# First mixer's parameter stage, attention probabilities and layer norms of a two-layer trunk: four edits to the order and the engines of small operations

## The chip, the cores and the metric

The kernel runs on one core of a Trainium2 chip. A core has five engines that run side by side, each through its own queue in a fixed order: TensorE (PE in the rows, its weight loads PEld) multiplies, VectorE (DVE), ScalarE (ACT) and GpSimd (POOL) work elementwise, and SyncE (SP) issues most of the transfers. Engines wait for each other by semaphores. The metric is the time of one execution on the device, in microseconds (us); lower is better. The time of the kernel before is the median of 3 runs.

## What is computed

Two layers over 512 tokens of width 1024, each a mixer and a mixture of experts, with a layer norm behind each of the four.

```python
for layer in range(2):
    mix = fox_s5_mixer(h, ...) if layer == 0 else mlstm_mixer(h, ...)
    h = layer_norm(ALPHA * h + mix, ln_g[layer, 0], ln_b[layer, 0])
    h = layer_norm(ALPHA * h + hier_moe(h, ...), ln_g[layer, 1], ln_b[layer, 1])

def fox_s5_mixer(x, ...):
    q, k, v, f_logit, u = split(x @ w_in)          # 512, 512, 512, 8, 512 columns
    att = forgetting_attention(q, k, v, f_logit + f_bias)   # 8 heads of 64
    y = gelu(s5_scan(u, ...))                      # 32 groups of 16 channels, 64 states
    y = y * sigmoid(y @ w_glu + b_glu)
    return concatenate([att, y]) @ w_out

# forgetting_attention: c = cumsum(log_sigmoid(f_logit)); s = q k^T / 8 + c_q - c_k, causal;
#                       p = softmax(s);  out = p v
# s5_scan: h_t = lam * h_{t-1} + B u_t,  y = Re(C h) + D u,  lam = exp(dt * a) complex
# layer_norm: (x - mean) * rsqrt(var + 1e-5) * g + b
```

## The kernel before

All large products are made of three passes over parts: each operand is split into a high part (ScalarE's cast, L213) and a low part (VectorE or GpSimd subtracts, L214), and `mm3` (L266 to L268) adds high x high, high x low and low x high. Weights come in pieces of 1 MB (`load_piece`); a piece is loaded into one raw buffer, split, and used. The tile framework gives out the buffers: tiles of one tag share a fixed number of slots ("t" has 5, "s5pw" 2, "raw" 1). A planner sets the order of each engine's queue when the program is built, by the order in the source among what it holds ready, so that an operation's place in the source is its priority; on the chip each queue runs in that order, and an operation that waits holds up those behind it.

`mixer0` (L389) runs the first mixer. It loads x, projects u (two pieces, L401 to L412) and stores it, and then traces `s5_params` (L413, body L542 to L671): VectorE computes, in some 150 small operations of 32 to 128 columns that depend on one another, the discretised S5 parameters. Within it `powers` (L625) builds the first eight powers of a complex number by doubling, 18 operations a call: once for the state (PR, PI; L641) and twice for a rotation (C_, S_; L656 to L662), whose tables only lines 752 to 757 read, on GpSimd. Behind it come the forget gate: its weights are loaded and split by `small_w` (L415, L357), 24 products make the gate's rows (`gate_rows`), and VectorE and ScalarE make log-sigmoid and its running sum (L420 to L424), which the attention scores read. Then the four S5 batches are traced as generators and v is projected (two pieces). A batch's first phase makes parameters and outer products (L685 to L705; for batch 0 on VectorE, for the others mostly on GpSimd), transposes them (L717), makes small products (L732, L733), and the rotation C, S of 512 columns (L752 to L757, GpSimd). The second phase (L762 to L782) applies rotation and scan, and makes y.

`fox_pair` (L464) runs two heads: q and k projection, and for each head and each block of 128 queries the scores (L482 to L486), the row maximum (L488, VectorE), the exponential with its row sum (L491, ScalarE), the reciprocal (L492) and the product with it (L493, both VectorE). Then TensorE transposes the probabilities (L500), which are split and multiplied by v.

`out_proj` ends a mixer: 4 blocks of 128 tokens, products, the residual, statistics (`ln_stats`), the router, and `ln_apply` (L295), which applies the norm in two halves of 512 columns, two operations each (L300, L301). The MoE follows. `moe` (L1269) ends it: for each of 4 token blocks the last experts' parts are added to the gathered row (L1284, with a row sum), then `ln_sums` (L303), a generator of three steps: the mean (L309); squares of both halves on ScalarE with row sums (L314), variance, `rstd` on GpSimd (a power, L281), mean times rstd (L319); and the normalisation: ScalarE scales (L323), VectorE multiplies by g (L324), VectorE or GpSimd adds b (L325, by `LN_POOL`), each by halves. The result goes to `done`: behind the first MoE the transposes and splits for the second mixer (L1041), at the end the stores (two for a block). Behind block 0 of the first MoE a weight piece is split whose two operations are placed behind `last_act` and `last_ln`.

Of the kernel before, what the change touches and what calls it, by code (L numbers as in the profile page):

```python
# [11 lines left out]
BF16 = mybir.dt.bfloat16  # L12
I32 = mybir.dt.int32
AF = mybir.ActivationFunctionType
ALU = mybir.AluOpType
# [5 lines left out]
EPS = 1e-5  # L21
# [4 lines left out]
QK_AT = 1, 3  # L26
LN_POOL = (), (0,), (0,), ()
NLAST = 2
# [23 lines left out]
class Trunk:  # L52
# [242 lines left out]
    def ln_apply(self, y, gb, mu, rs):  # L295
        V = self.nc.vector
        g, b = gb
        for i in range(2):
            h = np.s_[:, i * 512:(i + 1) * 512]
            V.scalar_tensor_tensor(y[h], y[h], mu, g[h], op0=ALU.subtract, op1=ALU.mult)  # L300
            V.scalar_tensor_tensor(y[h], y[h], rs, b[h], op0=ALU.mult, op1=ALU.add)  # L301

    def ln_sums(self, y, s, gb, pool):  # L303

        nc = self.nc
        V = nc.vector
        g, b = gb
        mu = self.sm("lnmu", [128, 1], bufs=4)
        V.tensor_scalar(mu, s[:, 0:1], s[:, 1:2], -1.0 / 1024, op0=ALU.add, op1=ALU.mult)  # L309
        yield  # L310
        q = self.sm("lns", [128, 2], bufs=4)
        for i in range(2):
            junk = self.t("t", [128, 512])
            nc.scalar.activation(junk, y[:, i * 512:(i + 1) * 512], AF.Square, bias=mu, accum_out=q[:, i:i + 1])  # L314
        ve = self.sm("lnve", [128, 1])
        V.tensor_scalar(ve, q[:, 0:1], q[:, 1:2], 1.0 / 1024, op0=ALU.add, op1=ALU.mult)
        V.tensor_scalar(ve, ve, EPS, None, op0=ALU.add)
        rs = self.rstd(ve)
        V.tensor_tensor(mu, mu, rs, op=ALU.mult)  # L319
        yield  # L320
        for i in range(2):
            h = np.s_[:, i * 512:(i + 1) * 512]
            self.last_act = nc.scalar.activation(y[h], y[h], AF.Identity, scale=rs, bias=mu)  # L323
            self.last_ln = V.tensor_tensor(y[h], y[h], g[h], op=ALU.mult)  # L324
            (nc.gpsimd if i in pool else V).tensor_tensor(y[h], y[h], b[h], op=ALU.add)  # L325
        yield
# [62 lines left out]
    def mixer0(self):  # L389
# [13 lines left out]
        for half in range(2):  # L403
# [4 lines left out]
            for c in range(2):  # L408
# [3 lines left out]
                nc.sync.dma_start(ud[half * 2 + c].rearrange("s p j -> p s j"), us)  # L412
        self.s5_params()  # L413

        fw = self.small_w("fw", 8)  # L415
        fps = self.gate_rows(fw, x, 8)
        fb = self.sm("gb", [8, 1], bufs=1)
# [46 lines left out]
    def fox_pair(self, pr, x, v, cneg):  # L464
# [7 lines left out]
        for hh in range(2):  # L472
# [4 lines left out]
            for qb in range(4):  # L477
# [14 lines left out]
                nc.vector.reciprocal(r, r)  # L492
                nc.vector.tensor_scalar(p_[:, :n], p_[:, :n], r, None, op0=ALU.mult)  # L493
                P.append(p_)
# [47 lines left out]
    def s5_params(self):  # L542
# [81 lines left out]
        V.tensor_scalar(ZI, ZI, -1.0, None, op0=ALU.mult)  # L624
        def powers(R_, I_):  # L625

            m = 1
            while m < 8:
                t1 = self.sm("s5pw", [128, 4, 32], bufs=2)[:, :m, :]
                t2 = self.sm("s5pw", [128, 4, 32], bufs=2)[:, :m, :]  # L630
                kr = R_[:, m:m + 1, :].to_broadcast([128, m, 32])
# [24 lines left out]
        for i in range(2):  # L656
            C_, S_ = keep(9), keep(9)
            nc.gpsimd.memset(C_[:, 0, :], 1.0)
            nc.gpsimd.memset(S_[:, 0, :], 0.0)
            V.tensor_copy(C_[:, 1, :], co)  # L660
            V.tensor_copy(S_[:, 1, :], ss)
            powers(C_, S_)  # L662
            co, ss = C_[:, 8, :], S_[:, 8, :]
            CS.append((C_, S_))
# [604 lines left out]
    def moe(self, layer, done):  # L1269
# [3 lines left out]
        for tb in range(6):  # L1273
            if tb < 4:
                x = self.xr[tb]
                s = self.sm("lnsm", [128, 2], bufs=4)
                for n in range(2):
                    ns = np.s_[n * 512:(n + 1) * 512]
                    ps = self.p("pj" if n == 0 else "mm", [128, 512])
                    for i in range(NLAST):  # L1280
                        for j in range(2):
# [3 lines left out]
                                                   accum_out=s[:, n:n + 1])  # L1285
                ln.append(self.ln_sums(x, s, gb, LN_POOL[tb]))
                next(ln[tb])
# [311 lines left out]
```

## Time and profile of the kernel before

| | |
|---|---|
| time, median of 3 runs | 1134.22 us (1133.0 to 1135.67) |
| profiled execution, its own time | 1129.98 us |
| its span | 1127.9 us |
| mean granted TensorE clock | 0.966 |
| TensorE busy | 1022.9 us, 91% |
| VectorE busy | 815.3 us, 72% |
| ScalarE busy | 559.5 us, 50% |
| GpSimd busy | 379.6 us, 34% |
| moved from and to memory | 180.62 MB, mean 160 GB/s |

The span runs from the first to the last instruction of the profiled execution; 2.1 us of its time lie around it. In it the first mixer takes about 310 us, the first MoE until about 560 us with its norms, the second mixer until about 870 us, and the second MoE the rest. All starts in the rows are in us from the span's start. In a row "out<-in" names the tile that is written and those that are read, buffer numbers left out; "[3.20 <-ACT pt L213]" says that the engine stood idle 3.20 us before it and what ended that. Busy TensorE is modelled time and not TensorE at its peak.

### The profile page before, as it was taken

How to read it: one execution, taken by the hardware profiler on the slowest of the kernel's cores; microseconds unless marked ns; L12 is line 12 of the kernel's file. 1: busy time of each engine (PE TensorE's matmuls, PEld its weight loads, DVE VectorE, ACT ScalarE, POOL GpSimd, SP SyncE). 2: the span in 40 equal slices, each digit the busy share in tenths (PEclk: the TensorE clock that was granted, in tenths of full speed). 3: DMA queues.
4: the chain of work that ended last, by engine and by line, in shares of the span. 5: the costliest groups of instructions: out<-in, count | busy, mean ns of one | idle time of the engine just before them, and what ended most of it. 6: DMA issues, size and time to landing. Idle time of an engine off the chain costs nothing. (4 is left out here: it accounts for less than half of the span.)

```text
span 1127.9 us, 14810 instructions
## 1 busy us (share of the span) xinstructions
PE 1022.9 (91%) x5522; PEld 826.9 (73%) x5522; DVE 815.3 (72%) x1485; ACT 559.5 (50%) x778; POOL 379.6 (34%) x226
## 2 busy tenths in 40 slices
PE   7879999999989999997699999999999899999872
PEld 5566767767768787875577989898777787877761
DVE  7886899778776776767665766667988767767666
ACT  5123554461445665664544444444424556666744
POOL 3077546001223333345243333331012233424352
PEclk9899999999989999999799999999999899999986
DMA  6313321541257786768622222221402577868684
GB/s 227 104 58 109 127 66 46 170 170 37 114 211 249 274 291 233 287 240 248 144 75 75 76 75 75 75 76 38 150 38 114 178 267 274 313 226 297 226 218 134
DMA packets 48347, 180.62 MB, mean 160 GB/s; under 512 B 17588, under 2 KB 18516, under 8 KB 32264
## 3 DMA queue, kind: packets, MB, share of 16 engines
q1 hardware_dynamic: 41240, 156.11, 39.4%
q0 software_dynamic: 2992, 8.77, 4.0%
q10 hardware_dynamic: 4032, 14.68, 3.2%
q8 instruction: 46, 0.75, 0.3%
q14 instruction: 37, 0.30, 0.1%
HBM read 155.94 MB, written 22.42 MB: 158 GB/s over the span
## 5 line engine op out<-in xcount | busy, mean ns | idle before, releaser
L266 PE MATMUL pj<-x,wh 128*128 128x512 f32 x288 | 116.6, 406 | 7.4 <-ACT x L213 5.7
L214 POOL TENSOR_TENSOR wl<-raw,wh 128x2048 fp32r<-128x2048 f32 x15 | 69.9, 4663 | 137.2 <-ACT wh L213 137.2
L267 PE MATMUL pj<-x,wh 128*128 128x512 f32 x288 | 115.5, 401 | 0.0
L214 POOL TENSOR_TENSOR wl<-ca,wh 128x2048 fp32r<-128x2048 f32 x16 | 75.1, 4692 | 119.9 <-ACT wh L213 97.5
L213 ACT CAST wh<-raw 128x2048 fp32r<-128x2048 f32 (+1 forms) x49 | 88.2, 1801 | 53.4 <-DMA raw<-in_w 40.0
L268 PE MATMUL pj<-x,wl 128*128 128x512 f32 x288 | 114.7, 398 | 0.0
L1073 PEld LDWEIGHTS tp<-t,a 128*128 128x128 f32 x896 | 110.8, 191 | 3.0 <-ACT pt L1065 0.6
L1073 PE MATMUL tp<-t,a 128*128 128x256 f32 x896 | 111.8, 283 | 0.0
L214 POOL TENSOR_TENSOR x<-ca,x 128x2048 fp32r<-128x2048 f32 x14 | 64.6, 4618 | 135.7 <-ACT x L213 106.2
L214 DVE TENSOR_TENSOR wl<-raw,wh 128x2048 fp32r<-128x2048 f32 (+1 forms) x34 | 72.8, 2140 | 39.6 <-ACT wh L213 39.3
L214 DVE TENSOR_TENSOR wl<-ca,wh 128x2048 fp32r<-128x2048 f32 x14 | 32.1, 2292 | 60.7 <-ACT wh L213 60.7
L1180 ACT ACTIVATE a<-mm,s5bc 128x512 f32<-128x512 f32 x56 | 38.5, 687 | 73.4 <-PE mm L268 73.4
L213 ACT CAST x<-ca 128x2048 fp32r<-128x2048 f32 (+1 forms) x40 | 66.1, 1651 | 12.3 <-DMA ca<-in_w 8.4
L266 PEld LDWEIGHTS pj<-x,wh 128*128 128x128 f32 x288 | 55.4, 192 | 19.7 <-ACT x L213 6.8
L267 PEld LDWEIGHTS pj<-x,wh 128*128 128x128 f32 x288 | 54.8, 190 | 12.0 <-DVE x L214 1.8
L213 ACT CAST wh<-ca 128x2048 fp32r<-128x2048 f32 x30 | 57.1, 1904 | 13.0 <-DMA ca<-in_w 12.9
L268 PEld LDWEIGHTS pj<-x,wl 128*128 128x128 f32 x288 | 55.1, 191 | 10.7
L1054 DVE TENSOR_SCALAR t<-iota,rcm 128x128 fp32r<-128x128 f32 x112 | 58.5, 565 | 0.4
L267 PE MATMUL pj<-wl,x 128*128 128x256 f32 x192 | 56.4, 294 | 0.9 <-DVE wl L214 0.9
L268 PE MATMUL pj<-wh,x 128*128 128x256 f32 x192 | 56.2, 293 | 0.1
L266 PE MATMUL pj<-wh,x 128*128 128x256 f32 x192 | 56.2, 293 | 0.0
L281 POOL TENSOR_TENSOR lnrs<-lnve,nhalf 128x1 f32<-128x1 f32 x16 | 13.1, 818 | 126.3 <-DVE lnve L292 99.7
(488 smaller groups left out, 2869.1 us busy)
## 6 DMA issues: line engine op xcount, KB each, us to landing
raw<-in_w SPq DMA_DIRECT2D x63, 1024.0 KB, 5.2
ca<-in_w SPq DMA_DIRECT2D x62, 1024.0 KB, 5.8
yd<-a ACTq DMA_DIRECT2D x28, 512.0 KB
a<-in_ln SPq DMA_DIRECT2D x8, 512.0 KB, 6.5
a<-in_w SPq DMA_DIRECT2D x6, 512.0 KB, 6.8
yd<-t SPq DMA_DIRECT2D x6, 512.0 KB, 3.1
ca<-in_xT SPq DMA_DIRECT2D x8, 256.0 KB, 5.7
xr<-in_x SPq DMA_DIRECT2D x4, 512.0 KB, 6.3
```

The lines of the kernel that those rows point to most:

```text
L213: a = nc.scalar.copy(h, src)
L214: b = (eng or nc.vector).tensor_sub(l, src, h.bitcast(F32))
L266: nc.tensor.matmul(ps, lhsT=aH[ai], rhs=bH[bi], start=first, stop=False)
L267: nc.tensor.matmul(ps, lhsT=aH[ai], rhs=bL[bi], start=False, stop=False)
L268: nc.tensor.matmul(ps, lhsT=aL[ai], rhs=bH[bi], start=False, stop=last)
L281: self.last_pow = self.nc.gpsimd.tensor_tensor(rs, ve, self.nhalf, op=ALU.pow)
L1054: ins = nc.vector.tensor_scalar(oh[:, j, m * 128:(m + 1) * 128], self.iota1, c[2 * i + j], None, op0=ALU.is_equal)
L1073: nc.tensor.matmul(tp[:, k, :], lhsT=self.xs[tb][i][:, cs], rhs=ohs[tb], start=tb + i == 0, stop=tb + i == 4)
L1180: nc.scalar.activation(yo[:, ns], ps, AF.Copy, scale=c)
```

## The change

Four edits. (1) In `mixer0` the load and split of the forget gate's weights are traced ahead of `s5_params` instead of behind it; the products and the rest of the gate stay behind. (2) In `s5_params` the two calls of `powers` for the rotation, and the two copies ahead of each, go from VectorE to GpSimd; their temporaries come from tag "t" (5 slots) in place of "s5pw" (2 slots). The call for the state's powers stays. (3) In `fox_pair` the product of the probabilities with the reciprocal goes from VectorE to ScalarE, a Copy with a scale. (4) The norms are applied at full width: `ln_apply` with two operations of 1024 columns in place of four of 512. In `ln_sums` one square of 1024 columns (into a bf16 scratch tile) takes the place of two; VectorE makes (y - mean) * g as soon as the square has read y; the variance takes one small operation; and the last step is one VectorE operation, y * rstd + b. ScalarE's scaling, the product of mean and rstd, and GpSimd's sums go. `last_act` now names the square and is set in the second step.

```diff
--- before.py
+++ after.py
@@ -24,7 +24,6 @@
 TWO_PI = 6.283185307179586
 S5_AT = 1, 1, 2
 QK_AT = 1, 3
-LN_POOL = (), (0,), (0,), ()
 NLAST = 2
 
 
@@ -295,12 +294,10 @@
     def ln_apply(self, y, gb, mu, rs):
         V = self.nc.vector
         g, b = gb
-        for i in range(2):
-            h = np.s_[:, i * 512:(i + 1) * 512]
-            V.scalar_tensor_tensor(y[h], y[h], mu, g[h], op0=ALU.subtract, op1=ALU.mult)
-            V.scalar_tensor_tensor(y[h], y[h], rs, b[h], op0=ALU.mult, op1=ALU.add)
-
-    def ln_sums(self, y, s, gb, pool):
+        V.scalar_tensor_tensor(y, y, mu, g, op0=ALU.subtract, op1=ALU.mult)
+        V.scalar_tensor_tensor(y, y, rs, b, op0=ALU.mult, op1=ALU.add)
+
+    def ln_sums(self, y, s, gb):
 
         nc = self.nc
         V = nc.vector
@@ -308,21 +305,15 @@
         mu = self.sm("lnmu", [128, 1], bufs=4)
         V.tensor_scalar(mu, s[:, 0:1], s[:, 1:2], -1.0 / 1024, op0=ALU.add, op1=ALU.mult)
         yield
-        q = self.sm("lns", [128, 2], bufs=4)
-        for i in range(2):
-            junk = self.t("t", [128, 512])
-            nc.scalar.activation(junk, y[:, i * 512:(i + 1) * 512], AF.Square, bias=mu, accum_out=q[:, i:i + 1])
+        q = self.sm("lns", [128, 1], bufs=4)
+        junk = self.t("t", [128, 1024], BF16)
+        self.last_act = nc.scalar.activation(junk, y, AF.Square, bias=mu, accum_out=q)
+        V.scalar_tensor_tensor(y, y, mu, g, op0=ALU.add, op1=ALU.mult)
         ve = self.sm("lnve", [128, 1])
-        V.tensor_scalar(ve, q[:, 0:1], q[:, 1:2], 1.0 / 1024, op0=ALU.add, op1=ALU.mult)
-        V.tensor_scalar(ve, ve, EPS, None, op0=ALU.add)
+        V.tensor_scalar(ve, q, 1.0 / 1024, EPS, op0=ALU.mult, op1=ALU.add)
         rs = self.rstd(ve)
-        V.tensor_tensor(mu, mu, rs, op=ALU.mult)
         yield
-        for i in range(2):
-            h = np.s_[:, i * 512:(i + 1) * 512]
-            self.last_act = nc.scalar.activation(y[h], y[h], AF.Identity, scale=rs, bias=mu)
-            self.last_ln = V.tensor_tensor(y[h], y[h], g[h], op=ALU.mult)
-            (nc.gpsimd if i in pool else V).tensor_tensor(y[h], y[h], b[h], op=ALU.add)
+        self.last_ln = V.scalar_tensor_tensor(y, y, rs, b, op0=ALU.mult, op1=ALU.add)
         yield
 
 
@@ -410,9 +401,9 @@
                 us = self.t("t", [128, 8, 64])
                 nc.scalar.copy(us, ps.rearrange("p (j s) -> p s j", s=8))
                 nc.sync.dma_start(ud[half * 2 + c].rearrange("s p j -> p s j"), us)
+
+        fw = self.small_w("fw", 8)
         self.s5_params()
-
-        fw = self.small_w("fw", 8)
         fps = self.gate_rows(fw, x, 8)
         fb = self.sm("gb", [8, 1], bufs=1)
         nc.sync.dma_start(fb, self.I["fb"])
@@ -490,7 +481,7 @@
                 r = self.sm("foxr", [128, 1], bufs=4)
                 nc.scalar.activation(p_[:, :n], sc[:, :n], AF.Exp, bias=mx, accum_out=r)
                 nc.vector.reciprocal(r, r)
-                nc.vector.tensor_scalar(p_[:, :n], p_[:, :n], r, None, op0=ALU.mult)
+                nc.scalar.activation(p_[:, :n], p_[:, :n], AF.Copy, scale=r)
                 P.append(p_)
             po = self.p("sm", [64, 512])
             for kb in range(4):
@@ -622,12 +613,12 @@
         V.tensor_tensor(a1, a1, a2, op=ALU.subtract)
         V.scalar_tensor_tensor(ZI, a1, sgn2, den, op0=ALU.mult, op1=ALU.mult)
         V.tensor_scalar(ZI, ZI, -1.0, None, op0=ALU.mult)
-        def powers(R_, I_):
+        def powers(R_, I_, V=V, tag="s5pw"):
 
             m = 1
             while m < 8:
-                t1 = self.sm("s5pw", [128, 4, 32], bufs=2)[:, :m, :]
-                t2 = self.sm("s5pw", [128, 4, 32], bufs=2)[:, :m, :]
+                t1 = self.t(tag, [128, 4, 32])[:, :m, :] if tag == "t" else self.sm(tag, [128, 4, 32], bufs=2)[:, :m, :]
+                t2 = self.t(tag, [128, 4, 32])[:, :m, :] if tag == "t" else self.sm(tag, [128, 4, 32], bufs=2)[:, :m, :]
                 kr = R_[:, m:m + 1, :].to_broadcast([128, m, 32])
                 ki = I_[:, m:m + 1, :].to_broadcast([128, m, 32])
                 V.tensor_tensor(t1, R_[:, 1:m + 1, :], kr, op=ALU.mult)
@@ -657,9 +648,9 @@
             C_, S_ = keep(9), keep(9)
             nc.gpsimd.memset(C_[:, 0, :], 1.0)
             nc.gpsimd.memset(S_[:, 0, :], 0.0)
-            V.tensor_copy(C_[:, 1, :], co)
-            V.tensor_copy(S_[:, 1, :], ss)
-            powers(C_, S_)
+            nc.gpsimd.tensor_copy(C_[:, 1, :], co)
+            nc.gpsimd.tensor_copy(S_[:, 1, :], ss)
+            powers(C_, S_, nc.gpsimd, "t")
             co, ss = C_[:, 8, :], S_[:, 8, :]
             CS.append((C_, S_))
 
@@ -1283,7 +1274,7 @@
                                              start=i + j == 0, stop=i == NLAST - 1 and j == 1)
                     nc.vector.scalar_tensor_tensor(x[:, ns], ps, 1.0, x[:, ns], op0=ALU.mult, op1=ALU.add,
                                                    accum_out=s[:, n:n + 1])
-                ln.append(self.ln_sums(x, s, gb, LN_POOL[tb]))
+                ln.append(self.ln_sums(x, s, gb))
                 next(ln[tb])
             if 0 < tb < 5:
                 next(ln[tb - 1])
```

## Rows read from the trace of the kernel before

**Rows 1.** The page's part 1: busy us (share of span) xinstructions.

```profile
PE 1022.9 (91%) x5522; PEld 826.9 (73%) x5522; DVE 815.3 (72%) x1485; ACT 559.5 (50%) x778; POOL 379.6 (34%) x226
```

**Rows 2.** TensorE's waits, 36 to 60, 60 to 80: total, times, longest.

```profile
PE sm L266 <- ACT pt L213: 3.2, 1, 3.2
PE sm L268 <- DVE pt L214: 1.9, 1, 1.9
...
PE tp L717 <- DVE xr L705: 3.0, 1, 3.0
PE sm L733 <- DVE xr L705: 4.0, 2, 3.3
```

**Rows 3.** TensorE by stretch: busy (instructions), granted clock, DMA share, GB/s.

```profile
43.00:50.00 7.00, 7.00 (x22) 0.65 0.41 151
```

**Rows 4.** Timeline, SyncE and ScalarE: start, us, engine line operation [idle before].

```profile
32.56 0.52 SPq L360 DMA_DIRECT2D t<-in_fw  x1
...
37.15 1.90 ACT L213 CAST wh<-raw 128x2048 fp32r<-128x2048 f32 x1 [9.69 <-DMA raw<-in_w]
...
39.43 0.25 ACT L213 CAST pt<-t 128x64 fp32r<-128x64 f32 x1
```

**Rows 5.** VectorE, 22 to 52, groups by shape: busy us, mean ns.

```profile
L633 DVE TENSOR_TENSOR s5pw<-raw 128x128 f32<-128x128 f32 x3 | 0.9, 286 | 0.1
...
L633 DVE TENSOR_TENSOR s5pw<-raw 128x32 f32<-128x32 f32 x3 | 0.6, 185 | 0.0
```

**Rows 6.** Timelines of GpSimd and VectorE; all engines from 36 to 78.

```profile
51.18 0.99 POOL L724 TENSOR_TENSOR s5pw<-ident,s5d 16x128 f32<-16x128 f32 x1 [30.14 <-DVE raw L638]
...
58.40 1.72 POOL L752 TENSOR_TENSOR s<-raw 128x512 f32<-128x512 f32 x1
...
76.63 0.40 POOL L689 TENSOR_TENSOR s5pw<-s5bc,raw 128x128 f32<-128x128 f32 x1
76.99 1.11 POOL L701 TENSOR_TENSOR xr<-raw,s5A 128x512 f32<-128x512 f32 x1
...
36.79 0.17 DVE L660 COPY raw<-s5t 128x32 f32<-128x32 f32 x1
...
58.84 1.84 DVE L705 TENSOR_TENSOR xr<-xr,pt 128x512 f32<-128x512 f32 x1
...
78.83 2.41 DVE L703 TENSOR_TENSOR pt<-raw,s5Aw 128x512 f32<-128x512 f32 x2 [3.65 <-POOL s5Aw L690]
...
81.76 1.28 DVE L705 TENSOR_TENSOR xr<-xr,pt 128x512 f32<-128x512 f32 x2
...
36.00:78.00 42.00, 29.71 (x197) 22.44 (x196) 35.06 (x79) 11.48 (x15) 20.74 (x19) 0.88 0.26 83
```

**Rows 7.** Lines 493, 491: ns min/median/max, first and last start; 110 to 240.

```profile
L493 DVE TENSOR_SCALAR t<-t,foxr x32: 254/422/1512, 107.8 to 232.5; 128x128 f32<-128x128 f32 x8, 128x256 f32<-128x256 f32 x8, 128x384 f32<-128x384 f32 x8, 128x512 f32<-128x512 f32 x8
...
L491 ACT ACTIVATE t<-mm,foxm x32: 351/532/692, 106.8 to 231.4; 128x128 f32<-128x128 f32 x8, 128x256 f32<-128x256 f32 x8, 128x384 f32<-128x384 f32 x8, 128x512 f32<-128x512 f32 x8
...
110.00:240.00 130.00, 124.07 (x720) 91.29 (x719) 110.02 (x226) 69.99 (x151) 49.00 (x47) 1.00 0.33 106
```

**Rows 8.** Lines 300 and 1197: the same operation, half and full width.

```profile
L300 DVE SCALAR_TENSOR_TENSOR xr<-xr,lnmv,a x16: 740/743/748, 257.9 to 866.5; 128x512 f32<-128x512 f32 x16
...
L1197 DVE SCALAR_TENSOR_TENSOR xr<-a,xr x8: 1207/1212/4797, 501.9 to 1072.2; 128x1024 f32<-128x1024 f32 x8
```

**Rows 9.** Behind the first MoE: TensorE's timeline, and all engines from 580 to 840.

```profile
554.34 1.12 PE L1041 MATMUL tp<-ident,xr 128*128 128x128 f32 x4 [5.86 <-DVE xr L325]
...
580.00:840.00 260.00, 257.07 (x1368) 215.64 (x1366) 182.75 (x258) 116.46 (x176) 66.57 (x16) 0.99 0.22 77
```

**Rows 10.** The end: VectorE's timeline, and all engines by stretch.

```profile
1109.38 0.69 DVE L1284 SCALAR_TENSOR_TENSOR xr<-pj,xr 128x512 f32<-128x512 f32 x1 [0.73 <-DMA xr<-yd,rsrc]
...
1123.09 1.28 DVE L325 TENSOR_TENSOR xr<-xr,a 128x512 f32<-128x512 f32 x2
...
1101.99:1124.37 22.38, 5.01 (x21) 3.49 (x19) 17.97 (x46) 11.83 (x24) 5.24 (x6) 0.67 0.45 124
```

## What the change is expected to do

> **What bounds the kernel now.** I read the busy shares first, then what TensorE waits for by stage, and then the stage around each edit. TensorE is busy for 1022.9 of 1127.9 us [rows 1], so an edit is worth what it takes out of TensorE's waits, or out of the end, where TensorE is already done. In the first 80 us it waits for four things [rows 2]: 3.2 us for the high part of the forget-gate weights, 1.9 us for their low part, and 3.0 and 4.0 us for the S5 products (L705). [...] The S5 stage is therefore worth at most 3.2 + 1.9 + 2.4 + 3.0 + 4.0 = 14.5 us. From 110 to 240 us, the attention, TensorE is busy for 124.1 of 130 us [rows 7], so at most 5.9 us can be won there. From 580 to 840 us it is busy for 257.1 of 260 [rows 9]: what is gained ahead of that stage is carried through it. At the very end VectorE is busy for 17.97 of 22.38 us [rows 10], while no product is left to run.
>
> **Part 1, forget-gate weights ahead.** The load was issued at 32.56 us and its high part was made only at 39.43, right behind a 1.90 us cast that had waited until 37.15 for another transfer [rows 4]. That first operation needs nothing of the S5 parameters, so an earlier place removes both waits and the clock loss, 7.5 us, if the load does get issued before the second v piece. The moved step issues one load (SyncE), one cast and one subtraction; they pass the S5 chain on VectorE, where the subtraction is one more small operation (0.2 us).
>
> **Part 2, rotation powers on GpSimd.** Two of the three sets of 18 operations leave VectorE. One set is six operations each at 0.286 us (128 wide), about 0.22 (64 wide, estimated between its neighbours) and 0.185 (32 wide) [rows 5], 4.1 us; two sets and four copies are about 9 us, and as they run back to back with some overlap I take 8 us off VectorE ahead of the S5 products of batch 0. GpSimd sat idle for 30.1 us up to 51.18 [rows 6], so it has room. Its price is not in the trace for 32 wide. A 128-wide product took 0.40 us undisturbed and a 512-wide one 1.11 [rows 6], a slope of 1.85 ns an element, so 0.28 for 64 and 0.22 for 32; 12 x (0.40 + 0.28 + 0.22) = 10.8 us, with four copies at 0.2 and some 0.05 between dependent operations 13.6 us. Disturbed it is longer: next to GpSimd's 1.72 us product at 58.40, VectorE's L705 took 1.84 us [rows 6], where two of the same line took 1.28 together at 81.76, with GpSimd idle [rows 6]. The two engines' products take turns. From 36 to 78 us VectorE ran 79 operations in 35.1 us [rows 6]; without the 40 that leave and the dozen small ones at its start, and undisturbed, I put what meets the rotation at 26 operations and some 16 us, so GpSimd's bounds are 13.6 and 13.6 + 16 = 29.6 us; I take the middle, 22. The rotation starts where its first copy stood, 36.79 [rows 6], and ends at 50 to 66, for me at 58.5. Its first reader on GpSimd, L752, began at 58.40 before [rows 6]: so the rotation tables C and S come no sooner and no later.
>
> [...]
>
> **What that leaves of the 14.5 us.** VectorE reaches batch 0's products 8 us or more earlier, so TensorE's 3.0 and 4.0 us waits go. But batch 1's parameters run on GpSimd behind L752 to L757, and there VectorE already waited 3.65 us at 78.83 (L703) for them [rows 6]. With C and S at the same time as before, batch 1's products are not earlier either. TensorE would arrive at batch 1's transposes up to 14.5 us early and must then do something else. What it has is pair 0's q and k projection, 48 products of 0.23 us spacing, 11 us, if the planned order puts them there. Bounds: 0 (it waits for batch 1) and 12. I take 5, because some of this projection already stood ahead of that point, and because nothing in the trace shows how the planner will order it. The chain of the forget gate now draws its "t" buffers behind the twelve that GpSimd's powers use, so VectorE's L420 may come some 5 us later; its reader, pair 0's scores, has its first exponential at 106.8 [rows 7], so I cost it at nothing. Queued behind L420 on VectorE are batch 0's products and the v parts: if that cover fails, it costs up to those 5 us, inside the bounds.
>
> **Part 3, probabilities by ScalarE.** 32 operations leave VectorE, median 0.422 us, 13.5 us in all; 32 come onto ScalarE, priced like its exponentials of the same widths, median 0.532 [rows 7], 17 us. ScalarE was busy for 70.0 of the 130 us, VectorE for 110.0 [rows 7]: there is room. Each new operation waits on ScalarE for VectorE's reciprocal, with casts out of PSUM queued behind it, for which TensorE waits. Gain at most some 2 us of the 5.9, loss at most some 32 x 0.1 = 3 us. I take 0.
>
> **Part 4, full-width norms in the middle.** Two halves of 0.743 us become one of 1.21 [rows 8], two such pairs in a block: 2 x (1.486 - 1.21) = 0.55 us on the last block's chain, in two layers: 1 us.
>
> **Part 5, norms behind the first MoE.** TensorE waited 5.86 us until 554.34 for block 0 [rows 9]. Its chain was two squares of half the width with their read-outs, two small operations, the power on GpSimd, another small one, ScalarE's scaling, product and sum. It becomes one square, a product of 1.21 that VectorE can do while it waits for a gather, one small operation, the power, and a last 1.21. That is about 1 to 3 us sooner, and the weights' low part behind it, too. I take 2.2; the stage from 580 us carries it [rows 9].
>
> **Part 6, the end.** The last gather lands at 1109.38; VectorE's last operation ends 15 us later, at 1124.37, and the store takes 3.5 us to 1127.9 [rows 10]. VectorE's work hardly changes: eight full-width operations (9.3 us at 1.16 spacing) for eight products and six sums (8.4). What goes is the detour over ScalarE and GpSimd's sums, for which VectorE stood idle 4.4 of the 22.38 us. [...] So 10.5 to 13.5 us in place of 15.0, minus 0.5 as the last store no longer goes in two steps: gain 1 to 4.5, I take 3.3.
>
> **The sum.** 5 + 0 + 1 + 2.2 + 3.3 = 11.5 us off the profiled execution's 1129.98, 1118.5. The median of the runs is 4.2 us above that execution; I carry it: 1123 us, with its own range 1117 to 1129.
>
> **Rivals.** (a) All of the S5 stage's waits go, for GpSimd ends its powers near 50 us and batch 1 moves up too: 12 in place of 5, 1116 us. For it: 30.1 us of idle GpSimd [rows 6]. Against: its products take turns with VectorE's. (b) The first mixer gives nothing, since TensorE only waits for batch 1 at a later place; the norms' 6.5 us remain: 1128 us. For it: the 3.65 us wait that is there already [rows 6]. (c) Slower: the powers and VectorE's 512-wide products take strict turns. Then each of 40 operations costs 0.40 + 0.60 = 1.0 us, the powers end near 77, and L752 is 18 us late. I let GpSimd's short gaps behind it give back 3; batch 1 and TensorE at its transposes are 15 us late, minus 6.5 from the norms: 1143 us. It is slower than before once the powers end after 58.4 + 3 + 6.5 = 68 us. Against: only 26 of VectorE's operations lie there, and some are small. (d) ScalarE's new waits hold up its casts: 5 us lost, 1128.
>
> **How the numbers follow.** Forecast 0.50, (a) 0.13, (b) 0.17, (c) 0.13, (d) 0.07. The predicted time is the first's, 1123. The range 1112 to 1134 takes in (a), (b), (d) and the outer ends of the forecast's terms, and leaves out (c) and a little of (a). A measurement of this kernel tells some 0.2%, 2.3 us, from no change: faster below 1132, slower above 1136.5. The forecast and (a), (b), (d) are faster for the most part, but a new order of the queues can cost some us anywhere: faster 0.77, same 0.09, slower 0.14.
>
> **What would show it.** L633 to L638 on GpSimd, the last ending at 55 to 62 us; the weights' first cast before 36 us and no wait of TensorE for it; L717 and L733 of batch 0 without a wait; TensorE's transposes behind the first MoE 1 to 3 us sooner after the gather; the last VectorE operation 10.5 to 13.5 us after the last gather. Powers that end after 68 us, or TensorE waiting over 5 us for batch 1, would make it wrong.

## The result, and the profile after

The changed kernel takes **1164.42 us** (median of 4 runs, 1163.11 to 1168.32) against 1134.95 for the kernel before beside it: a ratio of 1.0271, interval 1.0232 to 1.0311. It is 29.5 us slower; the forecast was 1123, with a range up to 1134. The profiled execution takes 1163.11 us, its span is 1161.4. Behind `ln_sums` its line numbers are 9 below those of before (L360 is L351, L705 is L696), and L213, L214 and L267 are L212, L213 and L266.

The page's first part, as [rows 1]: TensorE's products are the same, and it is busy for 20.7 us longer.

```profile
PE 1043.6 (90%) x5522; PEld 844.0 (73%) x5522; DVE 782.1 (67%) x1369; ACT 561.6 (48%) x778; POOL 388.2 (33%) x262
```

By milestones, before and after: the first softmax exponential starts at 106.8 and 114.8, the first tanh behind the attention (glu) at 232.1 and 267.5, the first dispatch product at 312.0 and 345.4, the last one at 880.2 and 918.1, and the spans end at 1127.9 and 1161.4. So **8 us are lost ahead of the attention, 27.4 in it**, some 6 at the last dispatch; some is given back at the norms.

Ahead of the attention: the waits from 60 to 84 us (engine, line, tile, releaser; total, times, longest), then GpSimd's and VectorE's timelines there.

```profile
PE pj L265 <- DVE a L213: 10.4, 1, 10.4
ACT t L374 <- POOL t L373: 10.2, 1, 10.2
DVE t L375 <- ACT t L374: 9.8, 1, 9.8
DVE pt L694 <- POOL s5Aw L681: 2.8, 1, 2.8
```

```profile
61.06 0.46 POOL L629 TENSOR_TENSOR raw<-t,t 128x128 f32<-128x128 f32 x1
...
63.35 2.10 POOL L743 TENSOR_TENSOR s<-raw 128x512 f32<-128x512 f32 x1
...
72.76 0.52 POOL L373 MEMSET t<- 128x512 f32 x1
...
77.14 0.45 POOL L681 TENSOR_TENSOR s5Aw<-s5Aw,s5pw 128x128 f32<-128x128 f32 x1
...
73.97 0.81 DVE L375 SCALAR_TENSOR_TENSOR t<-t,t 8x512 fp32r<-8x512 f32 x1 [9.78 <-ACT t L374]
77.62 2.18 DVE L694 TENSOR_TENSOR pt<-raw,s5Aw 128x512 f32<-128x512 f32 x2 [2.84 <-POOL s5Aw L681]
...
80.33 0.68 DVE L213 TENSOR_TENSOR a<-pj,a 128x512 fp32r<-128x512 f32 x1
```

GpSimd ends the powers at 61.5, within the 55 to 62 forecast, and goes on to the rotation tables (L743 to L748). Behind these stands the memset of the forget gate's row pair (L373), at 72.76; VectorE waits for it, then at L694 for batch 1's parameters, which come at 77.6 as they did before (78.8, [rows 6]). The value evacuation (L213: VectorE's part of moving a projected piece of v out of PSUM) stands behind both in VectorE's queue and starts at 80.33, and TensorE waits 10.4 us for it. In the kernel before it ran at 71.58, ahead of that product. Batch 0 did come earlier: TensorE's transposes for it (L708) run at 51.8 us without a wait, where they waited until 60.7 before; its products (L724) still wait 3.3 us, until 58.3 in place of 70.0.

In the attention, TensorE by stretch (busy, instructions, granted clock, DMA share, GB/s); the last row is the whole stage, first exponential to first tanh:

```profile
114.80:136.00 21.20, 21.20 (x111) 1.00 0.30 93
136.00:140.50 4.50, 2.23 (x10) 0.93 0.47 194
140.50:160.30 19.80, 18.54 (x65) 0.50 0.42 139
160.30:232.00 71.70, 67.50 (x397) 0.98 0.20 59
232.00:235.00 3.00, 1.87 (x9) 1.00 0.75 232
235.00:262.40 27.40, 27.36 (x96) 0.51 0.21 72
...
114.80:267.50 152.70, 143.80 (x704) 0.83 0.26 84
```

Before, the same stage was:

```profile
106.80:232.10 125.30, 119.76 (x699) 1.00 0.31 100
```

Against 1.00 before, the clock is at 0.50 for 19.8 us after one broken stretch (2.3 us idle of 4.5, in waits of 0.9 and 1.4) and at 0.51 for 27.4 us after another (1.1 of 3.0, in waits of 0.4 and 0.6), though TensorE is busy for 27.36 of these. The stage's length times its mean granted clock, its full-clock length, is 152.7 x 0.83 = 126.7 us; before it was 125.3 x 1.00. So nearly all of the 27 us are clock. The length of a wait doesn't tell its price: the longest of the stage, 3.2 us until 199.9 for a batch's transposes (L708), has only 6 us at 0.72 behind it.

Edit 1 shows on SyncE and ScalarE, as [rows 4]: the load goes out 8 us later than before, behind two others, and ScalarE waits for it.

```profile
40.45 0.53 SPq L351 DMA_DIRECT2D t<-in_fw  x1
...
43.63 0.24 ACT L212 CAST pt<-t 128x64 fp32r<-128x64 f32 x1 [3.48 <-DMA t<-in_fw]
```

The norms: TensorE's wait behind the first MoE, as [rows 9], is 4.9 us in place of 5.9, and VectorE ends 8.9 us after the last residual addition starts, in place of 15.0 [rows 10]. From the last gather's issue to the end of the span it is 25.5 us in place of 28.3.

```profile
PE tp L1032 <- DVE xr L316: 4.9, 1, 4.9
...
1148.40 0.69 DVE L1275 SCALAR_TENSOR_TENSOR xr<-pj,xr 128x512 f32<-128x512 f32 x1
...
1155.99 1.28 DVE L316 SCALAR_TENSOR_TENSOR xr<-xr,lnrs,a 128x1024 f32<-128x1024 f32 x1 [0.73 <-POOL lnrs L280]
```

At the start of the last expert stage a wait stands within one group of dispatch products, here first after and then before:

```profile
PE mm L1100 <- issue: 9.6, 1, 9.6
```

```profile
PE mm L1109 <- PEq L1211: 3.4, 1, 3.4
```

In both the branch of `overflow` (L1211 before, L1202 after) stands in TensorE's queue there, for 3.6 us before and 3.8 after. The other 6 us follow the branch, and nothing in the profile explains them.

### The profile page after: what moved, and what is told of

Read it like the earlier page. It is cut to its first block, busy times and chain, and to the rows that moved or that the text cites. A ratio compares the mean times of both kernels' runs of the same rounds, so it can differ in the third digit from the quotient of the medians.

```text
span 1161.4 us, 14713 instructions
## 1 busy us (share of the span) xinstructions
PE 1043.6 (90%) x5522; PEld 844.0 (73%) x5522; DVE 782.1 (67%) x1369; ACT 561.6 (48%) x778; POOL 388.2 (33%) x262
## 5 line engine op out<-in xcount | busy, mean ns | idle before, releaser
L266 PE MATMUL pj<-x,wh 128*128 128x512 f32 x288 | 116.4, 404 | 0.8 <-DVE x L213 0.8
L213 POOL TENSOR_TENSOR wl<-raw,wh 128x2048 fp32r<-128x2048 f32 x15 | 69.2, 4610 | 139.0 <-ACT wh L212 139.0
L267 PE MATMUL pj<-x,wl 128*128 128x512 f32 x288 | 114.9, 399 | 0.0
L213 POOL TENSOR_TENSOR wl<-ca,wh 128x2048 fp32r<-128x2048 f32 x16 | 74.2, 4637 | 117.2 <-ACT wh L212 103.0
L213 POOL TENSOR_TENSOR x<-ca,x 128x2048 fp32r<-128x2048 f32 x14 | 64.7, 4620 | 141.7 <-ACT x L212 108.4
L212 ACT CAST wh<-raw 128x2048 fp32r<-128x2048 f32 (+1 forms) x49 | 88.2, 1800 | 47.9 <-DMA raw<-in_w 33.4
L213 DVE TENSOR_TENSOR wl<-raw,wh 128x2048 fp32r<-128x2048 f32 (+1 forms) x34 | 74.6, 2193 | 40.7 <-ACT wh L212 40.7
L212 ACT CAST x<-ca 128x2048 fp32r<-128x2048 f32 (+1 forms) x40 | 66.0, 1651 | 14.6 <-DMA ca<-in_w 9.2
L213 DVE TENSOR_TENSOR wl<-ca,wh 128x2048 fp32r<-128x2048 f32 x14 | 32.1, 2292 | 59.7 <-ACT wh L212 59.7
L265 PE MATMUL pj<-wh,x 128*128 128x256 f32 x192 | 57.3, 298 | 13.7 <-DVE a L213 10.4
L280 POOL TENSOR_TENSOR lnrs<-lnve,nhalf 128x1 f32<-128x1 f32 x16 | 18.9, 1181 | 138.7 <-DVE lnve L291 106.7
L266 PEld LDWEIGHTS pj<-x,wh 128*128 128x128 f32 x288 | 55.3, 192 | 13.2 <-DVE x L213 3.0
L267 PEld LDWEIGHTS pj<-x,wl 128*128 128x128 f32 x288 | 55.3, 192 | 10.5
L212 ACT CAST wh<-ca 128x2048 fp32r<-128x2048 f32 x30 | 57.1, 1903 | 8.4 <-DMA ca<-in_w 8.3
L266 PE MATMUL pj<-wl,x 128*128 128x256 f32 x192 | 57.3, 299 | 0.0
L267 PE MATMUL pj<-wh,x 128*128 128x256 f32 x192 | 56.6, 295 | 0.0
```

The costliest lines, as they stand in the source:

```text
L212: a = nc.scalar.copy(h, src)
L213: b = (eng or nc.vector).tensor_sub(l, src, h.bitcast(F32))
L265: nc.tensor.matmul(ps, lhsT=aH[ai], rhs=bH[bi], start=first, stop=False)
L266: nc.tensor.matmul(ps, lhsT=aH[ai], rhs=bL[bi], start=False, stop=False)
L267: nc.tensor.matmul(ps, lhsT=aL[ai], rhs=bH[bi], start=False, stop=last)
L280: self.last_pow = self.nc.gpsimd.tensor_tensor(rs, ve, self.nhalf, op=ALU.pow)
```

## Experiments

Ratios are to the kernel before, run beside each, with 95% intervals; losses in us are worked out from them. "Stage" is the attention, first exponential to first tanh, in the run's trace, and "full-clock length" its length times its mean granted clock. Later runs build on earlier ones as told.

**The edits one at a time.** Each run is the kernel before with one hunk of the diff.

E1, ScalarE scaling:

> The kernel before with one edit alone: the probabilities are normalised by ScalarE instead of VectorE (all 32 of them). In the changed kernel the first softmax begins 8 us late and the first glu tanh 35 us late, so 27 us are lost between them. Theory 'ScalarE': the loss comes from this edit, which puts a wait for VectorE's reciprocal into ScalarE's queue 32 times, ahead of the exponentials and evictions behind it; then this run takes about 1155 to 1162 us and its first tanh begins 20 to 27 us later than before. Theory 'powers': the loss comes from the late and reordered S5 work that the moved powers bring; then this run is within 4 us of the kernel before (1131 to 1139).

Measured: 1140.66 us (1124 to 1142, 4 runs, too scattered for a ratio); stage 142.5 us at a clock of 0.87, full-clock length 124.0. The time is between the two theories. The planner's order is new here, too; E16 below holds the old one.

E2, powers:

> The kernel before with one edit alone: the two rotation-power passes and their four copies on GpSimd, temporaries in the general 512-column buffers, as in the changed kernel. Theory 'powers': the whole 35 us up to the glu come from it, so about 1162 to 1170 us (the norms' gain of some 6 us is missing here). Theory 'ScalarE': only the 8 us ahead of the first softmax are its own, so about 1140 to 1146. Both expect the zero rows' memset on GpSimd at about 73 us, VectorE's first value evacuation at about 80 and TensorE's wait of about 10 us for it.

Measured: 1158.56 us, 1.021 (1.0151 to 1.027), a little under theory "powers" and far over theory "ScalarE". Most of the loss is this edit's. The first exponential starts at 107.8, only 1 us late; the stage takes 151.9 us at 0.87 (full-clock length 132.2, so some 7 us of its loss are longer waits and not clock). TensorE's wait was there, but as 9.7 us for the gate's weights near 50, whose load waits while the powers' "t" tiles hold the gate's buffers: with a tile of their own for the powers, in E5, it is 3.2 us.

E3, all norms (the expectation's "middle" is the norm behind each mixer and behind the first MoE):

> The kernel before with one edit alone: full-width norms, both the middle one and the one at the end. By the changed kernel's milestones (2 us gained across the first expert stage, 5.5 us between the last gather result and the end) 1126 to 1129 us; by the prediction's terms (1 + 2.2 + 3.3 us) 1127 to 1131. A rival: the 6 us lost at about 906 to 918 us in the changed kernel belongs to this edit (the order of the second layer's start shifts with it), and this run then comes out at 1131 to 1135.

Measured: 1132.76 us, 1.0001 (0.997 to 1.0033). The rival was right: TensorE's long wait is here too, 9.3 us.

E4, gate weights ahead:

> The kernel before with one edit alone: the forget-gate weights' parts are asked for ahead of the S5 parameters. The prediction gave this 7.5 us. In the changed kernel the load was issued at 40.45 us instead of 32.56, not earlier. If the buffers the powers take were to blame for that, the load here is issued at or before 32.6 us and the run takes 1127 to 1131 us; if the load waits for a free 512-column buffer whichever statement stands first, it is issued at 32 to 41 us and the run is within 2 us of the kernel before.

Measured: 1134.64 us, 1.0003 (0.9976 to 1.0029). The load goes out at 32.59, 32.56 before [rows 4]: the statement's place doesn't move it.

**The two waits seen at 60 to 80 us.** E5 gives the powers a tile of their own; E6 also puts the memset on VectorE.

```diff
+        tmp = self.t("s2", [128, 8, 32])
...
-            powers(C_, S_)
+            powers(C_, S_, nc.gpsimd, tmp)
...
-        nc.gpsimd.memset(r.bitcast(F32), 0.0)
+        nc.vector.memset(r.bitcast(F32), 0.0)
```

> The kernel before with the rotation powers on GpSimd as in the run with the powers alone, but the temporaries in one tile of another pool (2 halves of it, reused, no wait between steps of one engine) and not in the five 512-column buffers that the forget gate's chain shares. Run with the powers alone: 1158.6 us, forget-gate bias add at 62.1, scan at 79.4, zero-row memset at 79.7, and TensorE at 0.50 of its clock from 109 to 150. Theory 'buffers': the powers held the gate's buffers; then the bias add comes at 50 to 52, the scan at 55 to 57, and nearly all of the 25 us goes (1130 to 1138). Theory 'GpSimd queue': the zero rows' memset stands behind the rotation tables on GpSimd and still comes at 70 us or later, the row pair with it, VectorE's value evacuation is held again and TensorE idles 5 to 10 us at 70 to 82, after which its clock falls; then 1142 to 1160. Theory 'port': GpSimd and VectorE slow each other whatever the buffers are; then the powers still end at 55 or later and the rotation tables begin no sooner than 63, and the time stays above 1145.

> As the run with the powers' own tile, and the zero rows' memset moved from GpSimd to VectorE besides, so that neither the buffers nor GpSimd's queue stand between the scan and the row pair. If these two are the whole mechanism, TensorE has no wait over 4 us between 60 and 110 us that the kernel before doesn't have, its clock is 1.00 over the attention stage and the time is 1124 to 1134 us: what is left then is the true worth of freeing VectorE, which the prediction put at 5 us. If GpSimd and VectorE disturbing each other carries it, the time stays above 1145.

Measured: E5 1159.18 us, 1.0236 (1.0167 to 1.0304); E6 1156.17 us, 1.0208 (1.0125 to 1.0292). In E5 the bias add (52.4) and the scan (58.1) come within about 1 us of theory "buffers", the memset (71.6) as late as "GpSimd queue" has it, and in E6 that is mended too; the time stays. So these two theories fall. The times are those of theory "port", that the two engines slow each other, over 1145 in both runs; E13 below decides on it. In E6 the gate's chain is within 2.3 us of before (row pair at 60.42, 58.12 before), and still VectorE's timeline shows:

```profile
60.42 0.89 DVE L384 SCALAR_TENSOR_TENSOR t<-t,t 8x512 fp32r<-8x512 f32 x1 [0.70 <-ACT t L383]
75.79 2.38 DVE L704 TENSOR_TENSOR pt<-raw,s5Aw 128x512 f32<-128x512 f32 x2 [14.48 <-POOL s5Aw L691]
78.10 0.68 DVE L214 TENSOR_TENSOR a<-pj,a 128x512 fp32r<-128x512 f32 x1
```

VectorE has nothing to do for 14.5 us but stands at batch 1's product, with the value evacuation behind it: the time that the powers freed turns into this wait, and TensorE waits 12.8 us. Batch 0 is early: its transposes run at 51.9 us and its products from 55.1, with 0.8 us of waits in place of 7.0.

**That order changed.** E9 is E6 with batch 1's first product behind the third value evacuation (in the kernel before it stands behind the second, other than the expectation says); E10 is the changed kernel with the three remedies.

```diff
-                self.split(vt[:, 0], vt[:, 1], ps)
+                self.vsub.append(self.split(vt[:, 0], vt[:, 1], ps)[1])
...
+                if b == 1:
+                    self.after(p, [self.vsub[2]])
```

> As the run with the powers' own tile and the memset on VectorE, and one thing besides: VectorE's first product of S5 batch 1 is put behind the third value evacuation in VectorE's order, as in the kernel before. In the run without it VectorE stood 14.5 us (61.3 to 75.8) at that product, waiting for a GpSimd product at the end of GpSimd's queue, with a value evacuation ready behind it since 66.1; TensorE waited 12.8 us for that evacuation (66 to 79). Theory 'order': the loss is this one place, and the rest (S5 late in the attention stage, TensorE's clock at 0.50 after short gaps there) follows from it; then TensorE has no wait over 5 us between 64 and 82, the first softmax begins at 100 to 107 (112.7 without), and the time is 1122 to 1135 us (1156 without). Theory 'GpSimd': what counts is that GpSimd ends its tables and batch 1's products late whatever VectorE does meanwhile; then the first softmax begins at 108 or later, or the attention stage still takes 140 us and more from first to last exponential (124.6 before), and the time is 1145 to 1158.

> The changed kernel whole, with three things undone or added: the powers' temporaries in a tile of their own, the zero rows' memset on VectorE, and VectorE's first product of S5 batch 1 behind the third value evacuation. Theory 'order': the 25 us of the moved powers go; what stays is the ScalarE edit (about 4 us by its own run) and nothing from the norms, so 1130 to 1140 us (1164 without). Theory 'GpSimd': 1150 to 1165.

Measured: E9 1146.33 us, 1.0134 (1.0058 to 1.0209); E10 1148.76 us, 1.0189 (1.0104 to 1.0274). About a third of the loss goes, with intervals that overlap E6's. By the times and by E9's stage theory "GpSimd" is ahead here, and E10 is just short of its range. In E9 the first exponential starts at 106.4, so the way there is worth what it was before, no more. The stage is still long, and its clock low (TensorE in E9 by stretch, the stage last; full-clock length 123.9):

```profile
104.00:123.00 19.00, 19.00 (x59) 0.55 0.27 87
139.00:157.00 18.00, 18.00 (x63) 0.53 0.54 176
106.40:253.90 147.50, 139.75 (x698) 0.84 0.27 86
```

**Work in the gaps.** E11 is E9 with matmuls whose results are overwritten, ahead of batches 1 to 3's transposes (two each) and outputs (one each). The first of the two places (dots for the rest of its line):

```diff
+            if b >= 1 and q == 0:
+                for _ in range(2):
+                    nc.tensor.matmul(tp.rearrange("p g j -> p (g j)"), lhsT=self.ident, rhs=C1...
```

> As the run with VectorE's order put right (1146 us), and with work for TensorE in the gaps that were left there: before the transposes of S5 batches 1 to 3 two matmuls (128x512, fp32) each, and before the output matmuls of each of these batches one more; their results are overwritten, nothing else is changed. In the run without them TensorE's granted clock was 0.50 at 105 to 122, 139 to 157, 177 to 184 and 201 to 208 us, each stretch after a gap of 1.5 to 2.5 us; these some 49 us at half speed account for the 22 us by which the attention stage is longer than before. Theory 'clock': with the gaps at 136 and 200 filled the clock stays at 1.00 after them, and the time falls to 1130 to 1141 though TensorE has up to 8 us more to do. Theory 'work': the attention stage is longer because its waits and its order are worse and the clock only goes along; then the time stays or rises: 1146 to 1156.

Measured: 1148.99 us, 1.0174 (1.012 to 1.0228). In the time theory "work" was right, in the stage theory "clock": behind 128 us the clock no longer falls, the three stretches are gone. But a new gap of 5.3 us opened at 104 and cost its own stretch, and the fillers are work (stage 139.6 us at 0.95, full-clock length 132.6). So the gaps' part in the low clock is supported and not proved, as the gaps changed in other places too:

```profile
104.00:109.00 5.00, 0.59 (x3) 0.87 0.14 29
109.00:128.00 19.00, 18.15 (x50) 0.50 0.25 83
128.00:254.50 126.50, 120.09 (x680) 1.00 0.28 89
```

**Order against place.** In E13 the powers are on GpSimd as in E6 and everything else up to the output projection stands in the order of the kernel before; E14 has the powers on VectorE and E9's order.

```diff
+        for e, text in ORDER.items():
...
+                if prev is not None:
+                    self.tc.add_manual_dep(i, prev.name, mybir.DependencyInfo(
+                        mybir.DependencyClass.NoSync, mybir.DependencyReason.DATA), reason="order")
+                prev = i
```

> The run with the powers on GpSimd, their own tile and the memset on VectorE (1156 us), with one difference: up to the output projection the instructions of each engine stand in the order that they have in the kernel before (edges of order alone, no waits); only the powers and their copies are placed freely in GpSimd's queue. Theory 'order': the powers' place costs nothing and the loss is that of the planner's new order; then the first softmax begins at 100 to 107, the attention stage takes 122 to 131 us from first to last exponential (124.6 before, 142 without), TensorE's clock stays at 1.00 in it, and the time is 1122 to 1133 us. Theory 'GpSimd': the powers' place costs it whatever the order; then 1145 to 1160.

> The reverse: the kernel before, powers on VectorE, nothing on GpSimd that was not there, with the instructions of each engine up to the output projection in the order of the run with VectorE's order put right (1146 us; the powers placed freely in VectorE's queue). Theory 'order': the loss is in that order: 1143 to 1160 us, with stretches of TensorE's clock at 0.50 in the attention stage. Theory 'GpSimd': without the powers on GpSimd the loss goes: 1126 to 1136.

Measured: E13 1131.02 us, **1.0004** (0.9979 to 1.0029); E14 1146.20 us, **1.0154** (1.0105 to 1.0203). In the traces TensorE and ScalarE run their instructions up to the first tanh exactly in the order of the kernel before in E13, and in that of E9 in E14. The stage in E13, then in E14 (full-clock lengths 124.4 and 124.9):

```profile
110.10:238.30 128.20, 122.91 (x699) 0.97 0.30 97
```

```profile
111.30:253.20 141.90, 134.19 (x697) 0.88 0.28 90
```

E6 and E13 differ in the order alone, 1.0208 against 1.0004. (The changed kernel's own "t" tiles were not run in the old order.) With the old order the place of the powers costs nothing and gains nothing; a new order alone, with no powers on GpSimd, costs 17 us. Two details fit less well. E13's first exponential starts at 110.1 us, outside theory "order" (100 to 107), and its clock is 0.97 and not 1.00; the last section shows how far the stage's clock differs between runs of one order. And part of E14's loss lies ahead of the stage: TensorE waits 11.5 us for the gate's weights there, 3.2 in E9.

**The norms.** E7 is `ln_sums` alone (used behind both expert stages, though its expectation speaks of the end only), E8 `ln_apply` alone (behind both mixers, though its expectation says otherwise), E12 is E8 again.

> The kernel before with the norms at the very end alone full-width (the norms behind the first expert stage as before). The run with both norms measured no gain: its end was 5.5 us shorter, but at about 880 us TensorE waited 9.3 us inside a group of matmuls where the kernel before waited 3.4, and 4 us were lost at the start, where both run the same instructions. Theory 'end alone': the wait of 9.3 us belongs to the other norms; then it is 3 to 4 us here and the run takes 1125 to 1129 us. Theory 'same': it belongs to the end's code, is 9 us here too, and the run takes 1130 to 1135.

> The kernel before with only the norms behind the first expert stage full-width. The prediction gave them 2.2 us (1 to 3), by transposes that begin sooner after the last gather. Theory 'end alone' of the run beside this one: TensorE's 9.3 us wait at about 880 us appears here, and the run is 3 to 7 us slower than before (1135 to 1140). Theory 'same': the wait is 3 to 4 us and the run takes 1129 to 1133.

> The kernel with only the norms behind the first expert stage full-width, once more and with more rounds: its first run gave 0.9953 of before, while its trace shows no gain at those norms (the last gather result to the first vector operation and to the first transposes as before, all 3 us late like everything before them). If the norms gain what the prediction gave them, 0.997 to 0.999 (2.2 us, 1 to 3); if the first run was chance, 0.999 to 1.002.

Measured: E7 1134.80 us, 1.0018 (0.9979 to 1.0058); E8 1129.23, 0.9953 (0.9917 to 0.9989); E12 1130.85, 0.9983 (0.9953 to 1.0013). The long wait goes with `ln_sums`: TensorE's waits at the last dispatch in E7 (in E8 it is 3.2 us):

```profile
PE mm L1102 <- PEq L1204: 3.3, 1, 3.3
PE mm L1102 <- issue: 5.1, 1, 5.1
```

E15 is E3 with four small matmuls at the start, so that TensorE's later instructions stand where they stood in its program.

```diff
+        wp = self.p("mm", [128, 128])
+        for _ in range(4):
+            nc.tensor.matmul(wp, lhsT=self.identb, rhs=self.maskqk, start=True, stop=True)
```

> The run with all norms full-width, and four small matmuls (128x128, bf16, nothing reads them) at the very start, where TensorE waits for its first weights anyway. In the programs run so far TensorE's wait at the start of the last expert stage was 9 us wherever 4692 to 4694 TensorE instructions stand ahead of that place and about 3.4 us wherever 4697 to 4702 do (the norms edit takes four to five away; here it is 4701). Theory 'place in the program': the wait is 3 to 4 us again and the run is 5 us faster than the run with all norms: 1123 to 1129, ratio 0.993 to 0.998. Theory 'norms': the wait stays at 9 us and the ratio at 0.999 to 1.002.

Measured: **1125.11 us, 0.9946** (0.9917 to 0.9976), faster than both kernels. The four matmuls alone, without the norms, were not run. The wait is back at its old length:

```profile
PE mm L1103 <- PEq L1205: 3.5, 1, 3.5
```

**ScalarE's scaling in the old order.** E16 is E1 with the order of before, as in E13.

> The kernel before with the probabilities scaled by ScalarE, and the instructions of every engine up to the output projection in the order of the kernel before; only the 32 scalings are placed freely in ScalarE's queue. The run with the edit alone and the planner's own order took 1140.7 in the median (1124 to 1142), its attention stage 142 us from first to last exponential in the trace against 124.6. Theory 'order': the stage takes 123 to 130 us and the run 1126 to 1133. Theory 'own waits': ScalarE's scalings hold the exponentials behind them, the stage takes 135 us or more and the run 1136 to 1145.

Measured: 1137.06 us, 1.0064 (1.0029 to 1.0099). The time is theory "own waits". The trace, taken from a short run (span 1131.2), is between the theories, and its stage of 131.2 us at 0.97 is hardly outside what runs of one order show (last section); its full-clock length, 127.3, is some 2 us more than theirs. TensorE's transposes wait 4.5 us for the scaling, 0.3 before.

```profile
107.00:238.20 131.20, 122.60 (x699) 0.97 0.29 95
```

```profile
PE tp L525 <- ACT t L518: 4.5, 4, 2.3
```

## Why the prediction was wrong

The step that failed is **"What that leaves of the 14.5 us"**: the planner's order was named there as unknown and still priced as a gain between 0 and 12, taken as 5. The runs show a loss in its place, and that it is the order's: the moved work is worth 0 us with the old order (E13) and costs 24 with the planner's (E2, and E6 with its two remedies), and one such order costs 17 without the moved work (E14). What the forecast had no term for is the clock behind a gap. It took 2.4 us for one known pause (the 7 us at 0.65 of [rows 3], 4.6 at full clock), but priced new gaps at their own length. That these 2.4 us, a part of its 14.5 and of Part 1's 7.5, would go with the pause no run shows: in the changed kernel TensorE still waits 3.1 us for the weights' high part, and the clock is 0.50 from 43 to 47. In the changed kernel's attention two stretches broken by waits of 0.4 to 1.4 us stand ahead of 47 us at half the clock, and the low clock makes up 26 of the 27.4 us lost. That the breaks are what lowers it is supported by E11 and not proved.

- **Part 1** (7.5 us, if the load is issued earlier): the condition failed. Alone the load keeps its place (E4), with the powers it is 8 us later.
- **Part 2**: the powers took 36.6 to 61.5 us, 58.5 forecast, and batch 1's parameters came no sooner, as forecast. VectorE was at batch 0 early, as forecast, and of TensorE's waits there the 3.0 us went and 3.3 of the 4.0 stayed. But what was freed became VectorE's wait for GpSimd (E6), and the value evacuation behind it TensorE's wait. The gain of 5 is 0, -3.3 to +2.4 (E13): rival (b)'s amount, though (b) had TensorE wait for batch 1 itself. The cover for the gate's chain, costed at nothing with 5 us if it failed, failed for 10.4 us of TensorE's time; where it holds, in E6, batch 1's product holds up the same evacuation, and the time is no better.
- **Part 3** (0, gain 2 to loss 3): a loss of 7 us, 3 to 11 (E16), rival (d)'s size. Its wait is another: (d) had ScalarE's casts held up, and in E16 TensorE's transposes wait 4.5 us for the scalings themselves and its products 0.9 for casts (0.3 before). The term counted the engines' busy time and not the chain of exponential, reciprocal and scaling that the transposes wait for.
- **Parts 4 to 6** (6.5 us): right in size, 6 us, 3 to 9 (E15). Behind the first MoE it is 1 us, not 2.2; VectorE ends 8.9 us after the last addition starts (10.5 to 13.5 forecast), for more of the norms was done ahead of it. No run shows the terms behind that range; GpSimd's power (L280), one for each of the four blocks at the end, took 0.57, 1.52, 1.46 and 0.55 us in the changed kernel. There all is lost again to TensorE's wait at the last dispatch, 6.2 us longer, which no step foresaw.
- **Rival (c)** had the sign but not the mechanism: the powers ended before 68 us. The sum as measured: 24 (E2) + 7 (E16) - 6 (E15) + 6 (the wait) = 31 of 29.5 us. The terms come from runs with different orders, so that they add up is no proof.

What a meeting of the two engines costs shows in the kernel before: VectorE's 512-wide product at 66.17 (L701) took 1.95 us and ended 0.56 us after GpSimd's beside it (L755, 1.79 us from 65.77), where two of them took 1.28 together with GpSimd idle [rows 6]. In the changed kernel a 128-wide power took 2.15 us at 57.02, beside VectorE's products, and 0.46 at 61.06, with VectorE idle. The powers ended at 61.5 and not at rival (c)'s 77, but (c) set a product of VectorE's beside each of the 40, and VectorE stood idle meanwhile for 3.7 us until 52.01 and for 3.6 until 56.98.

Open: why the same order gives low stretches in one run and none in another (below), and what in TensorE's program makes the wait at the last dispatch. It is 8.4 to 9.6 us in the four kernels with 4692 to 4694 TensorE instructions ahead of it (counted in the built programs) and 2.7 to 3.6 in those with 4697 or more. The four matmuls of E15, which nothing reads, brought it back from 9.3 to 3.5 us, so it hangs on the place of the instructions; by what mechanism was not tried.

## What to carry to other kernels

Where a planner orders the queues, moving an operation changes the order of everything around it: price that first, and to measure the move itself, hold the order of the kernel before. Time freed on an engine is worth something only if what it waits for next comes earlier too; look up that releaser before counting the gain. Behind a gap of TensorE in a dense stage the clock was low here for far longer than the gap (0.51 for 27.4 us behind waits of 0.4 and 0.6 us), so look at the granted clock there. And compare stages over several traces: one order's stage differed by 5.5 us from run to run.

## What the runs showed of the hardware

Behind a short gap the clock was low for many times the gap's length in the changed kernel (0.51 for 27.4 us behind 1.1 us of waits), and it is not so every time. The same product, in the same order, waited 1.43 us in the kernel before and in E13. First before, then E13 (timeline row, and the granted clock behind it):

```profile
158.06 0.44 PE L267 MATMUL sm<-pt,a 128*64 128x512 f32 x1 [1.43 <-DVE pt L214]
...
157.80:166.00 8.20, 7.94 (x46) 1.00 0.26 79
```

```profile
161.33 0.54 PE L277 MATMUL sm<-pt,a 128*64 128x512 f32 x1 [1.43 <-DVE pt L224]
...
162.00:166.00 4.00, 4.00 (x20) 0.63 0.08 15
```

Before, the clock stayed at 1.00; in E13 it was 0.63 over the next 4 us. What made the difference the profile doesn't show.

The same holds for the whole stage. E3, E7, E8 and E12 differ from the kernel before only behind the attention, and in their traces TensorE, VectorE and ScalarE run the same instructions in the same order up to the first tanh. Their stages took 129.4, 126.9, 130.8 and 128.2 us at clocks of 0.96, 0.99, 0.95 and 0.97, against 125.3 at 1.00 before; the full-clock lengths of all five are 124.2 to 125.6. E8's, for one:

```profile
106.20:237.00 130.80, 125.31 (x699) 0.95 0.29 95
```

So a stage's length in one trace can be 5 us off by the clock alone, with no edit behind it, and E13's 128.2 us can't be told from the kernel before. Stages are better compared by length times clock. The 23 runs of the kernel before beside E15 lie between 1120.9 and 1138.7 us at mean granted clocks of 0.955 to 0.966.
